# Mixer groups counted in column tiles, an input projection that begins 7 tiles wide, and the arithmetic ahead of it on VectorE alone

## The chip, the cores and the metric

One core of a Trainium2 chip runs the whole program in one launch. The metric is the device time of that launch in microseconds. Five engines work side by side, each on its own queue of instructions in a fixed order: TensorE (PE), VectorE (DVE), ScalarE (ACT), GpSimd (POOL) and SyncE (SP), which issues all of the kernel's DMAs. An instruction waits until what it reads is written and its target is free; what stands behind it on its engine waits with it.

## The reference

One layer of a decoder for 256 prompt tokens and 8 samples of one token each (264 columns), all in float32, with d_model 2048:

```python
h = h + 0.5 * rmsnorm(swiglu(rmsnorm(h, norm_ffn1_pre), ...), norm_ffn1_post)
mix, cb, xb, hs = token_mixer(rmsnorm(h, norm_mix_pre), ...)
h = h + rmsnorm(mix, norm_mix_post)
h = h + 0.5 * rmsnorm(swiglu(rmsnorm(h, norm_ffn2_pre), ...), norm_ffn2_post)
gate = jax.nn.sigmoid(rmsnorm(h, norm_ple_pre) @ w_ple_gate)
h = h + rmsnorm(gate * (p @ w_ple_proj), norm_ple_post)

def token_mixer(u, ...):
    glu_a, glu_b, z, xbc, dt_raw = split(u @ w_in)
    v = glu_a * sigmoid(glu_b)
    v, new_conv_buf = causal_dwconv(v, ...)             # 31 taps
    v = silu(layernorm(v, ...))
    xbc, new_xbc_buf = causal_dwconv(xbc, ...)          # 4 taps
    xs, bm, cm = split(silu(xbc))
    dt = softplus(dt_raw + dt_bias)
    y, h_new = ssd(xs, dt, -exp(a_log), bm, cm, d_skip, h0)   # 8 groups of 6 heads
    yg = y * silu(z)                                    # gate, RMSNorm in each group
    yg = yg * rsqrt(mean(yg * yg, per group) + EPS) * ssm_norm_g
    return concat(v, yg) @ w_out, ...
```

For the samples `ssd` is one step of the recurrence, from each sample's stored state `h0` of 48 x 64 x 128 numbers; for the prompt it runs in chunks of 128 tokens.

## The kernel before

**Matrix products.** Activations lie with features on the 128 partitions and the 264 tokens along the row, 16 tiles for d_model. Every product is made of three matmuls (`mm3`, L246): weight and activation are each split in a high half, rounded to fp32r, and the rest, and high x high, high x low and low x high are added in PSUM. The weights come as *units* in the order of `PLAN` (L71): two halves of 8 blocks of 128 x 128; each half is loaded (`wraw`), rounded on ACT (`whi`, L152) and subtracted on DVE (`wlo`, L153), at most two units ahead of use and with 4 buffers each. The activation's halves are written by `split` (L252), as tile `act`.

A *column tile* is one accumulator `acc` of 128 outputs: 16 k-tiles x 3 = 48 matmuls, one unit of weights. `gemm_one` (L346) does one; `gemm_first` (L334) starts a product four tiles wide, k by k, so that it can begin while the later activations are being made. `acc_ps` has 5 PSUM buffers, `ps` 3 for all else.

**The transition** (L487 to L523). When the first feed-forward block is done, three sums over partitions (`total`, L297) give the scale `rs`, and through `q2` the scale `r` of the mixer's input. For every k: `ys[k] * rs` (on GpSimd for the odd k above 2), addition to `H(k)` (on GpSimd but for k = 0), then the scalar form with `mix_pre` and `r`, and its split: `us`. The product with w_in follows these.

**The mixer's loop** (L810) goes over `IN_ORDER`, 81 column tiles: dt, then for each of 8 groups B, C, three x and three z, with a pair of GLU tiles in groups 1, 2, 4, 6 and the last four pairs behind the groups. `do_dt` (L552) ends in DMAs: dt and dt*a of the samples go to DRAM (`d_dt`) and come back spread over partitions (`dtp`, `eap`), and `eap` is exponentiated. `act` (L238) ties every ACT instruction that needs a function table to the one before in program order, so Silu and Exp keep the order in which they are written; a switch adds a table load (L236). `do_conv` (L610) makes B, C and x of an accumulator: three scalar forms on DVE, an addition, a Silu on ACT. `ssd` (L698) then does the group: transposes (L708), the chunked scan, and at its end the samples: the rows of B and C are transposed (L762, L763), copied (L765), stored (`d_bc`) and loaded again onto all partitions (`cbc`, L768); six pieces `h0` of the state (3 buffers) are loaded, multiplied by `cbc` on GpSimd, and reduced on DVE (L775) to `ych`. The `gate` (L790) of a group, y times Silu(z), squares added on GpSimd (`run`), their sum on PE (`total`, L300), normalisation and split, is called after the first x tile of the next group. `bg` holds the taps of the 31-tap convolution, 4 taken after each column tile.

**What sets the order.** The program is written in one sequence, and a scheduler puts each engine's instructions in a fixed order by priority (program order, unless `high_priority` moves a piece ahead) and by its own estimate of when operands are ready.

Of the kernel before, what the change touches and what calls it, by code (L numbers as in the profile page):

```python
# [19 lines left out]
P = 128  # L20
# [19 lines left out]
GLU_IN = (1, 2, 4, 6)  # L40
# [3 lines left out]
def _in_order():  # L44
# [26 lines left out]
def _plan():  # L71
# [18 lines left out]
    first = [m for _, m in IN_ORDER[:4]]  # L90
    for q in range(4):
        plan.append(("in", k16[4 * q : 4 * q + 4], first))
    for _, m in IN_ORDER[4:]:
# [32 lines left out]
class Weights:  # L126
# [9 lines left out]
    def load(self, between=()):  # L136
# [5 lines left out]
        with nullcontext() if between else tc.high_priority():  # L142
# [24 lines left out]
def kernel(ctx: ExitStack, tc: tile.TileContext, a: dict):  # L167
# [166 lines left out]
    def gemm_first(xs, kts, nunits):  # L334
        accs = [acc_tile() for _ in range(4)]
        n = 0
        total = nunits * 4
        for _ in range(nunits):
            w = ws.next()
            for kk in range(4):  # L340
                for m in range(4):
                    mm3(accs[m], w[4 * kk + m], xs[kts[n]], n == 0, n == total - 1)
                n += 1
# [12 lines left out]
    def ffn(xs, sq, done):  # L356
# [18 lines left out]
        accs = gemm_first(xs, k16, 4)  # L375
# [113 lines left out]
    rs = ffn_scale(ysq.total(), eq)  # L489

    q2 = tmp()
    tt(q2, yy.total(), rs, ALU.mult)
    stt(q2, hy.total(), 2.0, q2, ALU.mult, ALU.add)
    tt(q2, q2, rs, ALU.mult)
    stt(q2, eq, DM / EPS, q2, ALU.mult, ALU.add)
    r = rtile()
    rsqrt(r, q2, scale=1.0 / DM)
# [143 lines left out]
    def do_glu(i, pb, pa):  # L641
        if i < len(GLU_IN) + 2:
# [55 lines left out]
    def ssd(g, bf, cf, xt, ab, ea):  # L698
# [59 lines left out]
        tt(y[:, :, P:NP_], y[:, :, P:NP_], ea, ALU.add)  # L758

        js = slice(3 * g, 3 * g + 3)  # L760
# [5 lines left out]
        nc.sync.dma_start(d_bc[g].rearrange("i b n -> b i n"), rows[:NS])  # L766
        cbc = mp.tile([P, NS, P], F32, tag="cbc", bufs=1, name=nm("cbc"))
        nc.sync.dma_start(cbc, d_bc[g, 1].partition_broadcast(P))  # L768
        ych = mp.tile([P, 3, NS], F32, tag="ych", bufs=1, name=nm("ych"))
        for j in range(3):  # L770
# [368 lines left out]
```

## Time and profile before

| | |
|---|---|
| time, median of 3 runs | 2439.51 us (2439.47 to 2445.9) |
| the profiled execution | 2438.53 us, its span 2436.7 us |
| PE, DVE, ACT, POOL busy | 2370.0, 1577.0, 1181.7, 349.8 us |
| mean granted TensorE clock | 0.993 |
| DMA | 489.89 MB, 201 GB/s |

The share of the span in 40 equal slices of 61 us, in tenths; the mixer's tiles run from the thirteenth slice to the twenty-fourth:

```profile
PE   8999999999999999999999999899999999999988
DVE  6554455545557858979798975866555565565595
ACT  6444444433456465565655555544444443344464
POOL 2500000000015212121121011400000000000142
```

PE has work almost always; DVE is near its limit in some of the mixer's slices, GpSimd is mostly free, and ACT is at about half.

### The profile page before, as it was taken

Reading aid. Unit: us, or ns where it says so; the run is one execution under the profiler, and the core shown is the slowest. Engines: PE = TensorE matmul, PEld = TensorE weight load, DVE = VectorE, ACT = ScalarE, POOL = GpSimd, SP = SyncE. Lnnn points to the kernel's source line nnn. Section 1 sums busy time; section 2 is a strip of 40 time slices with the busy share of each in tenths; the row PEclk is TensorE's granted clock in tenths of the full one; section 3 lists DMA queues with packets and bytes.
Section 4 is the critical chain, followed back from the end, with each engine's and each line's share of the span. In section 5 each row is a group of like instructions: output and inputs, shape, how many; then the busy total and the mean of one; then the engine's idle time right before and its main releaser. Section 6 shows DMA issues by size and latency. Waiting matters only on the chain.

```text
span 2436.7 us, 47389 instructions
## 1 busy us (share of the span) xinstructions
PE 2370.0 (97%) x19444; PEld 2343.4 (96%) x19444; DVE 1577.0 (65%) x2273; ACT 1181.7 (48%) x1765; POOL 349.8 (14%) x351
## 2 busy tenths in 40 slices
PE   8999999999999999999999999899999999999988
PEld 8999999999999899999999999899999999999988
DVE  6554455545557858979798975866555565565595
ACT  6444444433456465565655555544444443344464
POOL 2500000000015212121121011400000000000142
PEclk9999999999999999999999999999999999999999
DMA  7656555555556666676666556477766676676653
GB/s 245 215 184 184 183 183 183 183 184 183 184 170 207 210 197 191 208 222 204 205 215 197 181 178 226 139 239 235 232 208 226 227 241 217 217 234 203 192 177 132
DMA packets 165386, 489.89 MB, mean 201 GB/s; under 512 B 25472, under 2 KB 42544, under 8 KB 165168
## 3 DMA queue, kind: packets, MB, share of 16 engines
q1 hardware_dynamic: 165168, 486.86, 62.1%
q8 instruction: 152, 2.49, 0.4%
q14 instruction: 66, 0.54, 0.1%
HBM read 465.65 MB, written 22.42 MB: 200 GB/s over the span
## 4 chain that ended last, share of the span: by engine, by line
PE 81%; DVE 7%; DMA 4%; issue 3%; ACT 2%; POOL 1%; SPq 0%; POOLq 0%; ACTq 0%; DVEq 0%
PE acc L248 26%; PE acc L249 26%; PE acc L250 26%; DVE wlo L153 3%; DVE y L217 1%; DMA d_bc<-rows 1%; DMA cbc<-d_bc 1%; POOL h L214 1%; DMA s<-in_hst 1%; DMA h<-in_hst 1%; DVE h L214 1%; DVE tmp L217 1%; ACT whi L152 1%; POOL run L214 1%; DVE act L217 1%
## 5 line engine op out<-in xcount | busy, mean ns | idle before, releaser
L250 PE MATMUL acc<-act,wlo 128*128 128x264 f32 x6320 | 1796.6, 285 | 4.4 <-DVE wlo L153 4.2
L249 PE MATMUL acc<-act,whi 128*128 128x264 f32 x6320 | 1783.7, 283 | 14.7 <-DVE act L217 7.8
L248 PE MATMUL acc<-act,whi 128*128 128x264 f32 x6320 | 1767.6, 283 | 16.6 <-ACT whi L152 8.7
L153 DVE TENSOR_TENSOR wlo<-wraw,whi 128x1024 fp32r<-128x1024 f32 (+1 forms) x806 | 994.9, 1236 | 584.9 <-ACT whi L152 580.7
L152 ACT CAST whi<-wraw 128x1024 fp32r<-128x1024 f32 (+1 forms) x806 | 829.0, 1033 | 945.2 <-PE acc L249 698.4
L248 PEld LDWEIGHTS acc<-act,whi 128*128 128x128 f32 x6320 | 1191.8, 190 | 19.9 <-ACT whi L152 8.9
L249 PEld LDWEIGHTS acc<-act,whi 128*128 128x128 f32 x6320 | 1188.6, 188 | 20.4 <-DVE act L217 10.0
L250 PEld LDWEIGHTS acc<-act,wlo 128*128 128x128 f32 x6320 | 1187.3, 188 | 8.1 <-DVE wlo L153 6.1
L214 POOL TENSOR_TENSOR run<-run,tmp 128x264 f32<-128x264 f32 x135 | 129.6, 960 | 956.0 <-ACT tmp L241 952.5
L214 POOL TENSOR_TENSOR s<-s,eap 128x1024 f32<-128x1024 f32 x24 | 46.4, 1932 | 598.8 <-DMA s<-in_hst 598.8
L217 DVE SCALAR_TENSOR_TENSOR y<-v,vec,y 128x251 f32<-128x251 f32 (+23 forms) x240 | 117.3, 512 | 1.2
L217 DVE SCALAR_TENSOR_TENSOR s<-bb,xds,s 128x128 f32<-128x128 f32 x192 | 52.6, 347 | 72.8 <-POOL s L214 72.8
L214 POOL TENSOR_TENSOR h<-h,cbc 128x512 f32<-128x512 f32 x48 | 72.2, 1524 | 167.4 <-DMA cbc<-d_bc 79.6
L256 ACT CAST act<-tmp 128x264 fp32r<-128x264 f32 x120 | 48.7, 411 | 72.8 <-DVE tmp L214 58.5
L214 DVE TENSOR_TENSOR tmp<-acc,rr 128x264 f32<-128x264 f32 x104 | 44.8, 431 | 56.8 <-PE acc L250 56.8
L214 DVE TENSOR_TENSOR tmp<-tmp,acc 128x264 f32<-128x264 f32 x88 | 37.7, 428 | 40.4 <-PE acc L250 39.4
L214 DVE TENSOR_TENSOR act<-tmp,act 128x264 fp32r<-128x264 f32 x120 | 54.3, 458 | 0.0
L241 ACT ACTIVATE tmp<-tmp 128x264 f32<-128x264 f32 x112 | 47.1, 422 | 10.2 <-DVE tmp L214 9.7
L241 ACT ACTIVATE tmp<-y 128x264 f32<-128x264 f32 x67 | 28.1, 426 | 43.6 <-DVE y L214 42.5
L214 DVE TENSOR_TENSOR y<-y,acc 128x264 f32<-128x264 f32 x80 | 34.0, 425 | 23.5 <-PE acc L250 23.5
L775 DVE TENSOR_REDUCE ych<-h 128x4 f32<-128x512 f32 x48 | 32.5, 678 | 20.0 <-POOL h L214 20.0
L217 DVE SCALAR_TENSOR_TENSOR act<-h,vec,act 128x264 fp32r<-128x264 f32 x48 | 35.2, 756 | 6.1 <-ACT act L241 6.1
(155 smaller groups left out, 787.2 us busy)
## 6 DMA issues: line engine op xcount, KB each, us to landing
wraw<-in_w SPq DMA_DIRECT2D x774, 512.0 KB, 4.7
h<-in_hst SPq DMA_DIRECT2D x48, 256.0 KB, 4.0
s<-in_hst SPq DMA_DIRECT2D x24, 512.0 KB, 6.8
out_nss<-s SPq DMA_DIRECT2D x24, 512.0 KB, 2.8
wraw<-in_w SPq DMA_DIRECT2D x32, 256.0 KB, 3.9
ab<-d_cs SPq DMA_DIRECT2D x16, 384.0 KB, 4.8
cbc<-d_bc SPq DMA_DIRECT2D x8, 512.0 KB, 4.3
bb<-d_bc SPq DMA_DIRECT2D x8, 512.0 KB, 8.3
```

What stands on the lines that cost most here:

```text
L152: nc.scalar.copy(hi, raw)
L153: nc.vector.tensor_tensor(out=lo, in0=raw, in1=hi.bitcast(F32), op=ALU.subtract)
L214: return (eng or nc.vector).tensor_tensor(out=out, in0=in0, in1=in1, op=op)
L217: return nc.vector.scalar_tensor_tensor(out=out, in0=in0, scalar=scalar, in1=in1, op0=op0, op1=op1)
L241: i = nc.scalar.activation(out=out, in_=in_, func=func, bias=bias, scale=scale)
L248: nc.tensor.matmul(acc, hi, x[:, 0, :], start=first, stop=False)
L249: nc.tensor.matmul(acc, hi, x[:, 1, :], start=False, stop=False)
L250: nc.tensor.matmul(acc, lo, x[:, 0, :], start=False, stop=last)
L256: nc.scalar.copy(t[:, 0, :], x)
L775: nc.vector.tensor_reduce(out=ych[:, j, b : b + 4], in_=h0, op=ALU.add, axis=AX.X)
```

## The change

It does five things.

1. The product with w_in begins with 7 column tiles instead of 4 (`FIRST_IN`), in 8 units of 2 k-tiles x 7 blocks. Two of the accumulators come from `ps`, five from `acc_ps`. The first seven tiles are dt, B, the three z of group 0, C and the first x: group 0's z moves ahead of its C.
2. Each group is an object `Group` whose steps are entered at column tiles counted from its C tile: the sample rows at C, `cbc` two tiles later, three thirds of the state's products (GpSimd) a tile apart from the third tile on, with the reductions of each third one step after its products; the scan a tile after the last x; the samples' result at C + 6 or two tiles after x; then the gate in two steps: the product with Silu(z) and the squares, and one tile later their sum and the rest.
3. GLU pairs stand in groups 1, 3 and 5, so that five are left behind the groups.
4. The transition's 15 additions and 7 multiplications on GpSimd go to DVE.
5. Priorities: the chain of scales after the first block has precedence, and so have the first two input tiles; the weight loads' priority is moved by a fixed offset of 1000.

```diff
@@
+FIRST_IN = 7
-GLU_IN = (1, 2, 4, 6)
+GLU_IN = (1, 3, 5)
@@ _in_order
+        z = [("z", MT_Z + 3 * g + j) for j in range(3)]
         out.append(("B", MT_BM + g))
+        if g == 0:
+            out.extend(z)
         out.append(("C", MT_CM + g))
         out.append(("x", MT_X + 3 * g))
         if g in GLU_IN:
             pair()
         out.extend(("x", MT_X + 3 * g + j) for j in (1, 2))
-        out.extend(("z", MT_Z + 3 * g + j) for j in range(3))
+        if g:
+            out.extend(z)
@@ Weights.load
-        with nullcontext() if between else tc.high_priority():
+        with nullcontext() if between else tc.high_priority(offset=1000):
@@ gemm_first
-        accs = [acc_tile() for _ in range(4)]
+        accs = [ps_tile([P, T]) if m < nm - 5 else acc_tile() for m in range(nm)]
@@ the transition
+    with tc.high_priority():
+        rs = ffn_scale(ysq.total(), eq)
...
+        rsqrt(r, q2, scale=1.0 / DM)
@@
-            tt(t, ys[k], rs, ALU.mult, nc.gpsimd if k % 2 and k > 2 else nc.vector)
-            tt(H(k), H(k), t, ALU.add, nc.gpsimd if k else nc.vector)
+            tt(t, ys[k], rs, ALU.mult)
+            tt(H(k), H(k), t, ALU.add)
         if k >= 2:
-            t = tmp()
-            stt(t, H(k - 2), V("mix_pre", k - 2), r, ALU.mult, ALU.mult)
-            us.append(split(t))
+            with tc.high_priority() if k < 4 else nullcontext():
+                t = tmp()
+                stt(t, H(k - 2), V("mix_pre", k - 2), r, ALU.mult, ALU.mult)
+                us.append(split(t))
@@ the samples, cut out of ssd
+    def sample_state(g, j, cbc, ych):
+        while products:
+            o, h0 = products.pop(0)
+            nc.vector.tensor_reduce(out=o, in_=h0, op=ALU.add, axis=AX.X)
+        if j == 3:
+            return
+        for b in range(0, NS, 4):
+            h0 = mp.tile([P, 4, P], F32, tag="h0", bufs=3, name=nm("h0"))
+            nc.sync.dma_start(h0, a["hst"][3 * g + j][:, b : b + 4, :])
+            tt(h0, h0, cbc[:, b : b + 4, :], ALU.mult, nc.gpsimd)
+            products.append((ych[:, j, b : b + 4], h0))
@@ gate, in two
+    def gate_begin(g, y, zs):
         tt(y, y, zs, ALU.mult)
         sq = SumSq(3, direct=0)
         for j in range(3):
             sq.add(y[:, j, :])
+        return sq
+
+    def gate_end(g, y, sq):
         t = tmp()
         rsqrt(t, sq.total(), eps1, 1.0 / 384)
@@ Group.__init__
+            at(place[("x", MT_X + 3 * g)], self.decays)
+            at(c, lambda: sample_rows(g, *self.pair()))
+            at(c + 2, self.sample_c)
+            for j in range(4):
+                at(c + 3 + j, lambda j=j: self.state(j))
+            at(x + 1, self.ssd)
+            out = max(c + 6, x + 2)
+            at(out, self.out)
+            begin = max(out, z) + 1
+            at(begin, self.begin)
+            at(begin + 1, self.end)
@@ the loop
-    first = gemm_first(us, k16, 4)
+    first = gemm_first(us, k16, 8, FIRST_IN)
...
+        for step in steps.pop(n, ()):
+            step()
```

Lines of the changed kernel's helpers lie 7 further down: `mm3` is L255 to L257 there, the `act` helper L248, the weight casts L159 and L160, `total` L307; the sample rows are transposed at L774 and L775 and reduced at L791.

**ACT, around the exponential of `eap`.** In these rows `eap`, `dte` and `cd` are results of `do_dt`, `bc` is B (and C) of group 0, `h` is x or z. Before:

```order
L591 COPY acs<-ps_9601 128x96
L599 COPY tmp_9613<-ps_9610 48x256
L241 ACTIVATE eap<-eap 128x192
L241 ACTIVATE dte<-dte 128x96
L241 ACTIVATE cd<-ps_9601 128x48
L236 ACT_TABLE_LOAD
L241 ACTIVATE bc_9616<-bc_9616 128x264 x2
L241 ACTIVATE h_9633<-h_9633 128x264
L236 ACT_TABLE_LOAD
```

And now:

```order
L625 COPY xo_9812<-acc_9869 128x11
L601 COPY acs<-ps_9796 128x96
L609 COPY tmp_9808<-ps_9805 48x256
L248 ACTIVATE eap<-eap 128x192
L248 ACTIVATE dte<-dte 128x96
L248 ACTIVATE cd<-ps_9796 128x48
L243 ACT_TABLE_LOAD
L248 ACTIVATE bc_9811<-bc_9811 128x264
L248 ACTIVATE h_9821<-acc_9331 128x264
L248 ACTIVATE h_9821<-acc_9332 128x264
L248 ACTIVATE h_9821<-acc_9333 128x264
```

Before, only the Silu of B and C and of the first x (`bc`, `h`) stand behind the exponential, and then a weight cast. Now the three z (read from their accumulators `acc`) stand there too.

**PE, behind the first pass.** `tm` and `tri` belong to `do_dt`. The first row below is the end of the eighth column tile (x, the second of group 0), which is the only one between the first pass and these rows. Waits are in brackets. Now:

```order
L257 MATMUL acc_9869<-act_9304,wlo_8_9668 128x264
L599 MATMUL ps_9796<-tm,tri 128x48 [waits DMAHW1_49,DMAHW7_49,Activation_49,Pool_49]
L600 MATMUL ps_9796<-tm,ones 128x48
L599 MATMUL ps_9796<-tm,tri 128x48
L600 MATMUL ps_9796<-tm,ones 128x48
L607 MATMUL ps_9805<-tri,tm 48x128 x2
L774 MATMUL ps_9832<-ident,bc_9811 8x128 [waits PE_49,Activation_49]
L255 MATMUL acc_9940<-act_9190,whi_0_9715 128x264 [waits Activation_49]
L256 MATMUL acc_9940<-act_9190,whi_0_9715 128x264
```

The transpose of B's sample rows (L774) and then the ninth column tile, whose accumulator is the first to be one that held a z, stand right behind that tile and the small matmuls of dt. Before, five column tiles and most of a sixth (B of group 1, below) stood between the first pass and L708, the transposes of x, the first that wait for such a Silu:

```order
L248 MATMUL acc_10098<-act_9262,whi_8_9982 128x264
L249 MATMUL acc_10098<-act_9262,whi_8_9982 128x264
L250 MATMUL acc_10098<-act_9262,wlo_8_9983 128x264
L708 MATMUL ps_9802<-ident,h_9633 128x128 [waits PE_49,Activation_49]
L708 MATMUL ps_9811<-ident,h_9633 128x128 [waits PE_49]
L722 MATMUL ps_9820<-bc_9616 128x128 [waits DVE_49]
```

**PE and DVE in the groups.** `run` is the sum of squares of a gate. The sum for group 1 and the sample rows of group 2 on PE, before (two places, the second 212 rows, or 4.4 tiles, later):

```order
L248 MATMUL acc_11603<-act_9278,whi_8_11356 128x264
L249 MATMUL acc_11603<-act_9278,whi_8_11356 128x264
L300 MATMUL ps_11171<-run_11162,ones 128x264 [waits Pool_49]
L708 MATMUL ps_11490<-ident,h_11153 128x128
L708 MATMUL ps_11499<-ident,h_11153 128x128 [waits PE_49]
```

```order
L248 MATMUL acc_11875<-act_9270,whi_8_11744 128x264
L762 MATMUL ps_11555<-ident,bc_11009 8x128 [waits DVE_49]
L763 MATMUL ps_11555<-ident,bc_11009 8x128
L249 MATMUL acc_11875<-act_9270,whi_8_11744 128x264
L250 MATMUL acc_11875<-act_9270,wlo_8_11745 128x264
```

and now:

```order
L255 MATMUL acc_11304<-act_9262,whi_8_11148 128x264
L307 MATMUL ps_11112<-run_11031,ones 128x264 [waits PE_49,Pool_49]
L774 MATMUL ps_11132<-ident,bc_11021 8x128 [waits PE_49]
L775 MATMUL ps_11132<-ident,bc_11021 8x128
L256 MATMUL acc_11304<-act_9262,whi_8_11148 128x264
L257 MATMUL acc_11304<-act_9262,wlo_8_11149 128x264
```

The rows come out right behind the sum. On DVE the first reductions of group 2 (`ych`) stand thus, before:

```order
L153 TENSOR_TENSOR wlo_0_11948<-wraw_0_11946,whi_0_11947 128x1024
L217 SCALAR_TENSOR_TENSOR y_11341<-v_11335,vec,y_11341 128x234
L217 SCALAR_TENSOR_TENSOR bc_11863<-acc_11875,vec,bc_11863 128x254
L775 TENSOR_REDUCE ych_11563<-h_622_11564 128x4
L217 SCALAR_TENSOR_TENSOR y_11341<-v_11335,vec,y_11341 128x233
L153 TENSOR_TENSOR wlo_8_11954<-wraw_8_11952,whi_8_11953 128x1024
L217 SCALAR_TENSOR_TENSOR bc_11863<-acc_11875,vec,bc_11863 128x253
L775 TENSOR_REDUCE ych_11563<-h_623_11568 128x4
```

and now:

```order
L224 SCALAR_TENSOR_TENSOR y_10484<-v_10478,vec,y_10484 128x228
L224 SCALAR_TENSOR_TENSOR y_10484<-v_10478,vec,y_10484 128x227
L791 TENSOR_REDUCE ych_11372<-h_598_11373 128x4
L224 SCALAR_TENSOR_TENSOR y_10484<-v_10478,vec,y_10484 128x226
L791 TENSOR_REDUCE ych_11372<-h_599_11376 128x4
L160 TENSOR_TENSOR wlo_8_11313<-wraw_8_11311,whi_8_11312 128x1024
L791 TENSOR_REDUCE ych_11372<-h_602_11444 128x4
```

Before, one reduction stood between two weight subtractions, with convolution taps around it; now two reductions stand ahead of one weight subtraction and a third behind it.

More of the change, by code (lines that the diff above doesn't have):

```diff
@@ L89, in _plan @@
         plan.append(("pp", [0, 1], list(range(8 * q, 8 * q + 8))))
[L90 to L93, printed above, removed]
+    first = [m for _, m in IN_ORDER[:FIRST_IN]]
+    for q in range(8):
+        plan.append(("in", k16[2 * q : 2 * q + 2], first))
+    for _, m in IN_ORDER[FIRST_IN:]:
         plan.append(("in", k16, [m]))
@@ L809, with at, last, group @@
+    steps = {}
+    def at(n, step):
+        steps.setdefault(n, []).append(step)
+    yctx = ctx.enter_context(ExitStack())
+    yp = None
+    def last():
+        nonlocal yp
+        mctx.close()
+        yp = yctx.enter_context(tc.tile_pool(name="yp", bufs=1))
+    first = gemm_first(us, k16, 8, FIRST_IN)
+    groups = {}
+    def group(g):
+        if g not in groups:
+            groups[g] = Group(g)
+        return groups[g]
     nglu = 0
     for n, (kind, m) in enumerate(IN_ORDER):
-        acc = first[n] if n < 4 else gemm_one(us, k16)
+        acc = first[n] if n < FIRST_IN else gemm_one(us, k16)
@@ L850 @@
                 bg.popleft()()
+    assert not steps
     for k in range(CM + 16, CM + 24):
```

110 lines of the change are left out of this document (58 added, 52 removed).

## The prediction

> **What bounds the kernel now.** I read the page first, then the windows around the one region that the diff touches, then PE's waits there.
>
> ```profile
> PE 2370.0 (97%) x19444; PEld 2343.4 (96%) x19444; DVE 1577.0 (65%) x2273; ACT 1181.7 (48%) x1765; POOL 349.8 (14%) x351
> PE 81%; DVE 7%; DMA 4%; issue 3%; ACT 2%; POOL 1%; SPq 0%; POOLq 0%; ACTq 0%; DVEq 0%
> L153 DVE TENSOR_TENSOR wlo<-wraw,whi 128x1024 fp32r<-128x1024 f32 (+1 forms) x806 | 994.9, 1236 | 584.9 <-ACT whi L152 580.7
> ```
>
> PE is busy for 2370.0 of 2436.7 us and carries 81% of the chain. The number of its matmuls does not change, so the change can only win or lose PE's stops and its half-clock stretches. The windows say where those are (columns: window; length, busy time of PE, PEld, DVE, ACT, POOL; granted clock; DMA).
>
> ```profile
> 760.00:780.00 20.00, 19.65 (x155) 18.83 (x153) 15.17 (x20) 13.76 (x25) 10.42 (x12) 1.00 0.65 205
> 780.00:800.00 20.00, 16.14 (x111) 15.31 (x110) 17.92 (x27) 13.22 (x30) 11.47 (x13) 0.91 0.87 289
> 800.00:820.00 20.00, 17.18 (x123) 16.44 (x122) 20.00 (x28) 8.34 (x15) 10.66 (x12) 0.91 0.60 209
> 820.00:840.00 20.00, 20.00 (x169) 20.00 (x168) 16.73 (x31) 11.64 (x23) 0.00 (x0) 1.00 0.61 199
> 840.00:900.00 60.00, 56.37 (x440) 53.69 (x439) 31.70 (x54) 37.52 (x74) 1.58 (x2) 0.94 0.61 178
> 900.00:1360.00 460.00, 442.85 (x3615) 428.78 (x3615) 393.66 (x678) 266.47 (x484) 96.95 (x74) 0.99 0.66 205
> ```
>
> At full speed PE starts 169 matmuls in 20 us: one each 0.118 us. I count a loss as idle time plus the clock's shortfall. **Transition** (760 to 820): 7.0 idle, and 0.09 of 40 us, is 10.6. **dt** (840 to 900): 3.6 idle and 0.06 of 60 is 7.2. **Mixer groups** (900 to 1360): 17.2 idle, and two dips of the clock, each 1.8 like that in the row of 780, make 20.8. Nothing else of PE's losses lies where the change reaches. Who PE waits for between 760 and 1360 us:
>
> ```profile
> PE ps L300 <- POOL run L214: 12.7, 9, 3.5
> PE acc L249 <- DVE act L214: 6.0, 4, 1.9
> PE ps L708 <- ACT h L241: 3.6, 2, 3.2
> PE acc L250 <- DVE wlo L153: 3.1, 4, 1.2
> ```
>
> A stop costs a little more than its row: the matmul before it drains for 0.28 us where its successor would have come at 0.118, so 0.16 each.
>
> **A. The transition: 7 column tiles wide, and GpSimd's arithmetic on DVE.** Four tiles wide, PE uses up one k-tile of the activations in 12 matmuls, 1.42 us; seven wide in 21, 2.48 us. What DVE takes for one:
>
> ```profile
> L153 DVE TENSOR_TENSOR wlo<-wraw,whi 128x1024 fp32r<-128x1024 f32 x17 | 23.7, 1393 | 3.1 <-ACT whi L152 3.1
> L217 DVE SCALAR_TENSOR_TENSOR tmp<-h,vec,rr 128x264 f32<-128x264 f32 x16 | 12.1, 761 | 0.0
> L214 DVE TENSOR_TENSOR act<-tmp,act 128x264 fp32r<-128x264 f32 x16 | 9.1, 596 | 0.0
> L214 POOL TENSOR_TENSOR h<-h,tmp 128x264 f32<-128x264 f32 x15 | 14.2, 954 | 6.1 <-DVE tmp L214 5.9
> 790.71 0.76 PE L248 MATMUL acc<-act,whi 128*128 128x264 f32 x4 [0.61 <-ACT act L256]
> 792.80 0.39 PE L249 MATMUL acc<-act,whi 128*128 128x264 f32 x1 [1.33 <-DVE act L214]
> 832.87 1.20 DVE L153 TENSOR_TENSOR wlo<-wraw,whi 128x1024 fp32r<-128x1024 f32 x1
> 834.01 0.47 DVE L217 SCALAR_TENSOR_TENSOR h<-acc,vec,h 128x255 f32<-128x255 f32 x1
> 834.40 0.14 DVE L214 TENSOR_TENSOR h<-h,shist 128x8 f32<-128x8 f32 x1
> ```
>
> These are the groups of 776 to 836 us, two rows of PE's timeline, and three of DVE's. Before: 0.76 + 0.60 + half a weight subtraction (0.70) is over 2.0 us against PE's 1.42, so PE must wait. After: 15 additions and 7 multiplications leave GpSimd, so that each k has three plain operations and one with a scalar, and 7/8 of a weight subtraction. From start to start, with GpSimd idle (820 to 840 above), DVE takes 1.14 for the subtraction and 0.39 for the scalar form (832.87, 834.01, 834.40); a plain one I take at 0.35, an estimate from these. That is 0.39 + 3 x 0.35 + 1.00 = 2.44, just under 2.48: PE is fed. The two operations that GpSimd did beside DVE are paid here, 0.70 a k, and the wider pass is what hides them; without it, 16 k-tiles would lose 16 x (1.95 - 1.42) = 8. What stays is the start. The first low half came at 792.80, after stops that sum to 1.9; now two more weight subtractions (2.3) stand ahead of it, and seven high-half matmuls in place of four cover 0.36 more: 3.9. With one half-clock window (3.4 us long, 1.7 lost) and the 0.6 of the first row that there was before, 6.2 remains of 10.6 plus 6 stops x 0.16, 11.6: **-5.4**. Bounds: -1, if DVE is a tenth slower (16 x 0.24 = 4), to -9, if the first stop stays as it was.
>
> **B. dt: a new wait.** The path of before, in the timelines of DVE, SP and ACT:
>
> ```profile
> 831.14 0.28 DVE L558 TENSOR_SCALAR h<-h 48x264 f32<-48x264 f32 x1
> 845.16 0.35 DVE L570 TENSOR_SCALAR h<-h,na 48x264 f32<-48x264 f32 x1
> 845.15 0.34 SPq L573 DMA_DIRECT2D d_dt<-h  x1
> 851.27 4.34 SPq L577 DMA_DIRECT2D eap<-d_dt  x2
> 859.99 0.36 ACT L241 ACTIVATE eap<-eap 128x192 f32<-128x192 f32 x1 [5.96 <-DMA eap<-d_dt]
> 860.63 1.28 ACT L236 ACT_TABLE_LOAD   x1
> 861.92 0.74 ACT L241 ACTIVATE bc<-bc 128x264 f32<-128x264 f32 x2
> 862.56 0.41 ACT L241 ACTIVATE h<-h 128x264 f32<-128x264 f32 x1
> ```
>
> From the store of dt to the exponential of `eap` lie 14.8 us of two DMA trips, and 2.3 more to the first Silu of B. ACT's order is fixed through that exponential: all Silu stand behind it. Before, PE had whole column tiles to run meanwhile, and stopped 3.2 us at the transposes L708. Now the three z tiles and B stand in those Silu, z holds three accumulators until then, and the transposes of the sample rows (L774) stand in PE's order right behind tile 7. So after the end E of the first pass PE has one tile only, of 48 x 0.12 = 5.8 us. E is followed by the operations of dt and the convolutions on DVE: 9 scalar forms (3.6), one weight subtraction (1.1), the reciprocal (1.7) and smaller ones, together some 7.3 us; plus 14.8 and 2.3 gives E + 24.4, and the Silu of the first z follows at once. PE has run 5.8 and 0.6 of small matmuls of it: 18 idle. Afterwards a part of the clock's next window, 2.5 lost (the 0.06 of 60 us above was 3.4 after a 3.2 us stop). 20.5 less 7.2 is **+13.3**. Bounds: +9, if the two trips take their landings alone (11 us), to +24, if dt's steps on DVE, of which the first can come at E + 3.7, spread over the 14.0 us that they took before (831.14 to 845.16).
>
> **C. The gates leave the critical path.** Eight of the nine waits of L300, 12.4 us and 8 x 0.16, belong to the sum of squares that PE reaches before GpSimd has added it. The product with z now stands one tile (5.8 us) ahead of its sum. In PE's order I count 2.1 to 2.8 tiles from the product to the sum where there were 1.5 to 1.8; the longest need before, its lead plus its stop, was 2.15. Groups 0 and 7 keep about 0.95 each: 13.7 to 1.9, **-11.8**, and the two dips of the clock that they caused, **-3.6**. Bounds: -8 (half the waits stay) to -17.
>
> **D. What is late next.** The sample rows leave PE right behind that sum, and the first reduction of the GpSimd products stands in DVE's queue a tenth of a tile after, where 0.85 tile lay between. In group 5 of before:
>
> ```profile
> 1196.95 0.27 PE L762 MATMUL ps<-ident,bc 128*8 128x128 f32 x1
> 1197.76 0.30 SPq L766 DMA_DIRECT2D d_bc<-rows x1
> 1202.64 0.34 SPq L768 DMA_DIRECT2D cbc<-d_bc x1
> 1208.17 0.69 DVE L775 TENSOR_REDUCE ych<-h 128x4 f32<-128x512 f32 x1 [0.79 <-POOL h L214]
> 1209.35 1.21 DVE L153 TENSOR_TENSOR wlo<-wraw,whi 128x1024 fp32r<-128x1024 f32 x1
> L214 POOL TENSOR_TENSOR h<-h,cbc x48: 1281/1302/2354, 899.2 to 1332.8; 128x512 f32<-128x512 f32 x48
> ```
>
> Rows to first reduction: 11.2 us, nearly all of it two DMA trips and one GpSimd product, which nothing here shortens. Behind the waiting reduction on DVE stands the weight subtraction of the next tile but one, and behind it PE. In groups 2 to 7 PE needs it 1.9 to 2.2 tiles after the rows, 11.5 to 13 us; it is done at 11.2 + 0.6 + 1.14 = 12.9, and with a second product (1.3) ahead of it at 14.2. I get 4 to 5 us in group 2 (two reductions ahead, row shown in the order above), 1.3 to 2.5 in groups 3 to 6, 2.5 in group 7, and 1 for groups 0 and 1: **+14**. The four old waits of wlo go, 3.1 + 0.6: **-3.7**. For the clock I take two windows, **+3.6**. Bounds of all this: -4 to +22.
>
> ```profile
> 1166.00:1176.00 10.00, 7.80 (x51) 7.48 (x50) 7.23 (x10) 7.07 (x12) 2.96 (x2) 0.83 0.80 252
> 980.00:990.00 10.00, 8.70 (x71) 8.37 (x70) 10.00 (x19) 6.71 (x14) 1.99 (x2) 1.00 0.69 225
> L236 ACT ACT_TABLE_LOAD  x27: 1283/1283/1283, 0.8 to 2423.2; - x27
> ```
>
> These windows say what a stop does to the clock: 2.2 us idle took it to 0.83 over the 10 us, 1.3 us idle left it at 1.00. So I expect it of the stops in groups 2 and 7 and not of the others. The Trainium skill, "TensorE: Matmul & The Clock Gate", section "Why this matters for your kernels", asks more: one idle window, about 3.4 us, before the clock halves. By that rule group 7's stop costs no clock, and the sum would be 1.8 lower; the row of 1166 to 1176 speaks against it.
>
> **Edits at nothing.** Twelve more table loads, 12 x 1.28 = 15.4 us on ACT, spread over the groups, where ACT is busy 266 of 460 us: hidden, at worst +3 where one stands ahead of a weight's cast. The scale's precedence moves a chain of some 3 us that the rows put ahead of 790.7 already: 0, at best -1. Two DMAs more on SP, and the longer priority offset of the weight loads, change the order of issues but no wait of PE that the rows show: 0. The last GLU convolutions: five pairs behind the groups in place of four, so 30 more DVE operations of 0.4 us, 12 us, later on; the sums of the layer norm still stand four units (24 us) ahead of their first use: 0.
>
> **Sum.** -5.4 + 13.3 - 11.8 - 3.6 + 14 - 3.7 + 3.6 = +6.4, on the profiled execution's 2438.5 us (span 2436.7, and 1.8 around it that stay): 2444.9. The median of 2439.5 is 1.0 above that execution, so I say **2446**.
>
> **The rivals.** (1) *The reductions never hold up PE*, since DVE has cleared its queue when they come due. For it: DVE is busy 394 of 460 us only. Against: the queue is in order, and the 11.2 us are DMA time. D falls to -3.7: 2446 - 14 - 3.6 = 2428. (2) *dt stays mixed with weight work on DVE.* In before its steps took 14.0 us on DVE, with a weight subtraction between nearly every two. For each microsecond that they end behind E + 7.3, PE idles one more, and from E + 8.1 on the result is over 0.3% slower; at E + 17.7 it is 2456. Against: the order now has one subtraction inside it, where seven stood. (3) *The gates are still waited for*, because the additions on GpSimd queue behind products of the samples, 1.3 us each and up to 2.35 while DVE works: then C gives 4 in place of 15.4, 2457. (4) *Short stops leave the clock alone*, as the cited rule has it for a stop under a window, and group 2's falls under it if its two reductions split it: no window in D, 2442.
>
> **Chances.** Forecast 0.42 (0.24 of it within 0.3%, 0.18 slower, since it lies close to that bound), rival 1 0.17 (0.14 faster), rival 2 0.18 (slower), rival 3 0.13 (0.10 slower), rival 4 0.10 (within). 0.3%, 7.3 us, is about what a measurement of this kernel can tell from no change: 2432.2 to 2446.8. Faster 0.14, same 0.40, slower 0.46. The range leaves out the lower half of rival 1 and the upper parts of 2 and 3: 2429 to 2458; that of the forecast alone is 2440 to 2452.
>
> **What would show it.** A: between 795 and the end of the first pass, near 835, PE without stops on DVE. B: one stop of 14 us or so on L774 or on the matmul behind it, ended by an ACT Silu. C: the waits of the total on GpSimd at 2 us or less. D: PE waits on wlo of 10 us or more, and reductions that wait for GpSimd right ahead of them. Wrong would be a stop in B under 8 us, or wlo waits that stay near 3.

## The result, and the profile after

The changed kernel takes 2454.61 us (median of 8 runs, 2451.8 to 2467.84) where the kernel before, on the same chip, takes 2440.84 (8 runs, 2436.42 to 2445.9): a ratio of 1.0064, 95% interval 1.0049 to 1.0079. The profiled execution is the longest of the eight, 2467.84 us with a span of 2466.1; what sets it apart comes below. From its page, and the windows that answer to those of before:

```profile
PE 2385.3 (97%) x19444; PEld 2360.7 (96%) x19444; DVE 1571.4 (64%) x2297; ACT 1197.0 (49%) x1779; POOL 327.9 (13%) x329
PE 88%; DVE 4%; ACT 3%; DMA 3%; issue 2%; POOL 1%; SPq 0%; ACTq 0%; POOLq 0%; DVEq 0%
L160 DVE TENSOR_TENSOR wlo<-wraw,whi 128x1024 fp32r<-128x1024 f32 (+1 forms) x808 | 991.3, 1228 | 611.9 <-ACT whi L159 604.8
...
780.00:800.00 20.00, 17.29 (x127) 16.08 (x125) 15.66 (x30) 15.52 (x35) 4.51 (x5) 1.00 0.84 285
800.00:820.00 20.00, 18.33 (x130) 18.33 (x131) 20.00 (x47) 8.78 (x15) 0.00 (x0) 0.83 0.69 231
840.00:860.00 20.00, 13.94 (x98) 13.07 (x96) 12.66 (x21) 7.61 (x18) 0.00 (x0) 0.91 0.46 115
860.00:880.00 20.00, 13.13 (x88) 12.86 (x89) 3.47 (x10) 15.28 (x33) 0.00 (x0) 0.74 0.51 134
900.00:1380.00 480.00, 454.00 (x3633) 439.67 (x3632) 391.94 (x675) 285.40 (x505) 86.26 (x68) 0.96 0.63 197
```

By the measure of the prediction, idle time and the clock's shortfall, the transition (780 to 820) loses 4.4 + 3.4 = 7.8 us, dt (840 to 880) 12.9 + 7.0 = 19.9, and the groups 26.0 idle and about 19 of clock (0.04 of 480, rounded). Before, the three were 10.6, 7.2 and 20.8. The three have grown by 34 us by this measure, and by 23 in the table below; in part, half clock while PE stands still is counted twice here, so the table is the better price. PE's waits between 740 and 1400 us of the changed kernel:

```profile
PE acc L257 <- DVE wlo L160: 21.5, 7, 5.3
PE ps L774 <- ACT bc L248: 8.8, 1, 8.8
PE ps L307 <- POOL run L221: 4.5, 3, 2.7
PE acc L255 <- ACT tmp L248: 4.1, 1, 4.1
```

The sum of the gates (L307) has fallen from 12.7 to 4.5; the wait for B's Silu at L774 and the one behind the first pass are new; and the waits for weight subtractions, 3.1 before, are now the largest.

To see where time goes without a window's edges, I count PE's weight matmuls from the start, 48 to a column tile, and take the time at which PE has done 132 tiles' worth (the first block), 140 (two tiles of another small product, then six tiles' worth of the product with w_in; in the changed kernel PE runs the seventh and last of the first pass behind this without a stop), 150 (dt is done) and 220 (behind all groups and five tiles further). The table gives each stretch's length less that of the kernel before, in profiled executions; GLU tiles stand in other places in the two, so each stretch is good to about 1 us. "Time" is the median of the runs, "ratio" that against the kernel before, measured beside it.

| kernel | to 132 | 132-140 first pass | 140-150 dt | 150-220 groups | rest | time | ratio (95%) |
|---|---|---|---|---|---|---|---|
| changed | +6.8 | -4.9 | +10.4 | +17.8 | -1.0 | 2454.6 | 1.0064 (1.0049-1.0079) |
| same_again | -0.5 | -4.8 | +9.7 | +8.2 | -1.3 | 2450.1 | 1.0053 (1.0036-1.0070) |
| dt_exp_later | +7.2 | -5.3 | +5.6 | +8.8 | -1.3 | 2450.9 | 1.0053 (1.0037-1.0070) |
| reduce_later | -0.2 | -4.7 | +10.1 | +1.5 | -0.8 | 2442.2 | 1.0016 (1.0003-1.0028) |
| both_later | -0.2 | -4.4 | +6.3 | -2.1 | -0.8 | 2441.7 | 1.0012 (1.0000-1.0024) |
| gate_only | +1.0 | -0.1 | +0.6 | +0.6 | -0.9 | 2438.7 | 1.0011 (0.9996-1.0026) |
| first_acc | -0.4 | -4.3 | +1.1 | +0.2 | -1.0 | 2437.1 | 1.0001 (0.9987-1.0014) |
| four_wide | -0.2 | -2.5 | +3.2 | +9.6 | +0.5 | 2449.5 | 1.0053 (1.0039-1.0068) |
| gpsimd_back | -0.5 | -4.8 | +10.1 | +8.2 | -1.2 | 2457.5 | 1.0086 (1.0055-1.0117) |
| no_trip | +8.0 | +3.7 | +11.0 | -9.1 | -2.1 | 2445.7 | 1.0032 (1.0020-1.0045) |
| early_only | -0.6 | -4.6 | -0.8 | +7.0 | -1.5 | 2439.8 | 1.0008 (0.9997-1.0019) |
| all_groups | +8.2 | -5.2 | +1.7 | +0.1 | -1.3 | 2435.0 | 0.9996 (0.9984-1.0007) |
| all_groups_exp8 | -0.2 | -5.4 | +1.2 | -0.5 | -1.3 | 2430.8 | 0.9972 (0.9961-0.9982) |

The first column is not the change's: it lies ahead of everything that was edited, and four executions have 7 to 8 us there and the others none (see the last section). So a single profile's total says less than its columns.

### The profile page after: what moved, and what is told of

Its sections match the earlier page's. It is cut to its first block, busy times and chain, and to the rows that moved or that the text cites. A ratio compares the mean times of both kernels' runs of the same rounds, so it can differ in the third digit from the quotient of the medians.

```text
span 2466.1 us, 47412 instructions
## 1 busy us (share of the span) xinstructions
PE 2385.3 (97%) x19444; PEld 2360.7 (96%) x19444; DVE 1571.4 (64%) x2297; ACT 1197.0 (49%) x1779; POOL 327.9 (13%) x329
## 4 chain that ended last, share of the span: by engine, by line
PE 88%; DVE 4%; ACT 3%; DMA 3%; issue 2%; POOL 1%; SPq 0%; ACTq 0%; POOLq 0%; DVEq 0%
PE acc L257 29%; PE acc L256 29%; PE acc L255 28%; DVE wlo L160 1%; DMA ab<-d_cs 1%; ACT ab L248 1%; ACT whi L159 1%; DMA cbc<-d_bc 1%; DVE tmp L224 1%; PE ps L759 0%; DVE act L224 0%; POOL h L221 0%; PE ps L744 0%; DMA wraw<-in_w 0%; PE ps L307 0%
## 5 line engine op out<-in xcount | busy, mean ns | idle before, releaser
L257 PE MATMUL acc<-act,wlo 128*128 128x264 f32 x6288 | 1796.7, 287 | 22.7 <-DVE wlo L160 22.6
L255 PE MATMUL acc<-act,whi 128*128 128x264 f32 x6288 | 1770.3, 284 | 18.9 <-ACT whi L159 8.5
L160 DVE TENSOR_TENSOR wlo<-wraw,whi 128x1024 fp32r<-128x1024 f32 (+1 forms) x808 | 991.3, 1228 | 611.9 <-ACT whi L159 604.8
L159 ACT CAST whi<-wraw 128x1024 fp32r<-128x1024 f32 (+1 forms) x808 | 829.1, 1030 | 994.6 <-PE acc L256 729.5
L257 PEld LDWEIGHTS acc<-act,wlo 128*128 128x128 f32 x6288 | 1187.7, 189 | 27.2 <-DVE wlo L160 25.1
L255 PEld LDWEIGHTS acc<-act,whi 128*128 128x128 f32 x6288 | 1190.9, 190 | 22.6 <-ACT whi L159 8.7
L256 PEld LDWEIGHTS acc<-act,whi 128*128 128x128 f32 x6288 | 1188.5, 189 | 11.5 <-DVE act L224 9.9
L224 DVE SCALAR_TENSOR_TENSOR y<-v,vec,y 128x243 f32<-128x243 f32 (+23 forms) x240 | 108.5, 482 | 0.6
L791 DVE TENSOR_REDUCE ych<-h 128x4 f32<-128x512 f32 x48 | 32.5, 676 | 31.0 <-POOL h L221 31.0
L248 ACT ACTIVATE tmp<-tmp 128x264 f32<-128x264 f32 x112 | 47.1, 421 | 10.2 <-DVE tmp L221 10.1
L248 ACT ACTIVATE tmp<-y 128x264 f32<-128x264 f32 x67 | 28.0, 425 | 42.9 <-DVE y L221 41.8
```

The source lines that it names most:

```text
L159: nc.scalar.copy(hi, raw)
L160: nc.vector.tensor_tensor(out=lo, in0=raw, in1=hi.bitcast(F32), op=ALU.subtract)
L224: return nc.vector.scalar_tensor_tensor(out=out, in0=in0, scalar=scalar, in1=in1, op0=op0, op1=op1)
L248: i = nc.scalar.activation(out=out, in_=in_, func=func, bias=bias, scale=scale)
L255: nc.tensor.matmul(acc, hi, x[:, 0, :], start=first, stop=False)
L256: nc.tensor.matmul(acc, hi, x[:, 1, :], start=False, stop=False)
```

## The experiments

**same_again.** The changed kernel once more, nothing edited.

> The changed kernel unaltered, for a second profile and for the spread. If the profiled execution of 2467.8 us was one with more stops than usual in the mixer groups, a second one of about 2454 shows the same stop of 14 us in the dt step (the sum of both stops 12 to 15) and fewer or shorter waits for wlo (under the 21.5 us of the first profile), or fewer dips of the clock. If the two agree within 3 us in every stretch, the spread lies elsewhere. Time 2452 to 2458.

2450.07 us. Its windows, and its waits from 740 to 1400 us:

```profile
820.00:900.00 80.00, 67.59 (x526) 65.46 (x525) 47.95 (x79) 42.03 (x81) 11.32 (x7) 0.91 0.63 187
900.00:1380.00 480.00, 456.40 (x3712) 442.97 (x3713) 401.80 (x700) 291.05 (x514) 87.89 (x68) 0.98 0.62 200
...
PE acc L257 <- DVE wlo L160: 20.5, 8, 5.3
PE ps L774 <- ACT bc L248: 8.3, 1, 8.3
PE ps L307 <- POOL run L221: 3.3, 3, 2.5
```

The waits are those of the first profile to within 1.2 us each. What the first had more is the clock's loss in the groups, 0.96 there and 0.98 here, and the 7 us ahead of the change: of what was expected, it is the fewer dips of the clock. I take this execution as the one to compare with from here on.

**dt_exp_later** writes the exponentials behind the Silu of B and z.

```diff
 def do_dt(acc):
-        act(eap, eap, AF.Exp)
...
-        act(dte, dte, AF.Exp)
-        act(cd, pc[:, 1, 1, :], AF.Exp)
+        exps.append(pc)
...
+    at(6, dt_exps)     # the three of them, ahead of group 0's decays
```

> The exponentials of eap, dte and cd are written six tiles later, at the first x of group 0, behind the Silu of B, C and the three z; nothing else changes. Theory (PE waits in the dt step because those Silu stand behind the DMA trips of eap): the wait of 8.8 us at L774 goes, PE's loss between 840 and 880 falls from 18 to 20 us to 4 to 8, and the time by 10 to 14, to 2441 to 2445. Rival (PE would wait there anyway, for the accumulators that dt and the convolutions hold): loss stays over 14, time 2451 to 2456.

2450.94 us: no gain in the time. PE's waits from 740 to 900 us, and the window beside that of same_again above:

```profile
PE acc L255 <- ACT tmp L248: 4.1, 1, 4.1
PE acc L257 <- DVE wlo L160: 3.4, 1, 3.4
PE ps L724 <- ACT h L248: 1.3, 1, 1.3
...
820.00:900.00 80.00, 71.19 (x554) 69.14 (x555) 56.06 (x91) 44.89 (x86) 10.51 (x7) 0.96 0.64 196
```

The wait at L774 is gone, as the theory has it, and the loss from 820 to 900 fell from 12.4 + 7.2 to 8.8 + 3.2 us, 7.6 less. But a wait for a weight subtraction and one for x came in its place (the dt stretch of the table is shorter by 4.1 only), and the groups keep their 8 to 9. The expected 10 to 14 was wrong. The time says no gain; in this profile 7.2 of its us lie ahead of the change, so about 4 us of gain is what the profile shows and the time cannot confirm.

**reduce_later** writes the products and reductions one tile later.

```diff
-                at(c + 3 + j, lambda j=j: self.state(j))
+                at(c + 4 + j, lambda j=j: self.state(j))
...
-            out = max(c + 6, x + 2)
+            out = max(c + 7, x + 2)
```

> The state's products and reductions are written one tile later in each group (from the fourth tile after C, not the third), and the samples' result with them. By the order the next weight subtraction behind a first reduction is then needed 2.9 to 4.2 tiles after the rows in groups 3 to 7 (2.2 to 2.4 before), and 2.2 in group 2. Theory (reductions at the head of DVE's queue hold the weight subtraction that PE needs): PE's waits for wlo fall from 21.5 us to under 6, dips of the clock with them, and the time by 12 to 22, to 2433 to 2443. Rival (the gate, which now follows a tile later, becomes the wait, or weights are late for another reason): waits for wlo under 8 but those of the sum L307 over 10, or wlo waits over 15; time 2450 to 2458.

2442.18 us, 8 below the changed kernel; the groups went from +8.2 to +1.5.

```profile
PE acc L257 <- DVE wlo L160: 10.0, 6, 6.6
PE ps L718 <- ACT h L248: 4.1, 4, 1.7
PE ps L307 <- POOL run L221: 4.1, 6, 1.2
```

The waits for wlo halved, and their longest, 6.6, is in group 2, which by the order had not moved (2.2 tiles). The gain is under the 12 to 22 expected: x (L718) waits 4.1 us that it did not before. The theory stands, its size does not.

**both_later**, the two edits together.

> Both edits at once. If the two losses are separate, as the first theories have it, the gains add: 22 to 36 less than the changed kernel, 2419 to 2432, which is faster than the kernel before by 0.4 to 0.9%. If removing one only lets the other take its place, the gain is no more than the larger of the two alone.

2441.67 us. Dt +6.3, groups -2.1: in the profile both gains are there, but the time is that of reduce_later alone. It did not reach the 2419 to 2432 expected. The 4 us that dt_exp_later wins in its stretch are at the limit of what these runs tell.

**gate_only** takes the kernel before, and puts a tile between a gate's squares and their sum.

```diff
             if j == 0:
-                finish_gate()
+                begin_gate()     # product and squares
                 ab, ea = decays(g)
+            elif j == 1:
+                finish_gate()    # sum, normalisation, split
```

> The kernel before, with one part of the change alone: a gate's product with Silu(z) and its squares stay where they were, and their sum on PE and the rest follow one column tile later. Where the sample rows and reductions stand does not change. Theory (the waits of the sum for GpSimd were worth 13.7 us and two dips of the clock, and the reductions cost the changed kernel what it won here): PE's waits at L300 between 900 and 1360 fall from 12.4 us to under 4, those for wlo stay near 3, and the time is 9 to 16 below the kernel before, 2422 to 2430. Rival (any delay of the gate brings the waits elsewhere, to x or the next wlo): gain under 4.

2438.65 us, 1.0011 of the kernel before: no change.

```profile
PE ps L300 <- POOL run L214: 8.8, 7, 2.1
PE acc L250 <- DVE wlo L153: 6.2, 7, 1.9
```

The sum's waits fell by 3.9 only, from 12.7, and those of wlo rose by 3.1. In five of the eight groups the product with Silu(z) still starts only 3.9 to 4.4 us ahead of its sum (3.6 to 5.0 in the kernel before), so there the edit did not make the distance it was written to make. It does not tell what the gates are worth alone, but it is a first case of one wait that takes the place of another.

**first_acc** is both_later with three of the first seven accumulators in the small pool.

```diff
-        accs = [ps_tile([P, T]) if m < nm - 5 else acc_tile() ...
+        accs = [ps_tile([P, T]) if m < nm - (4 if nm > 4 else 5) else acc_tile() ...
```

> Both later edits, and three of the first seven accumulators come from the small PSUM pool in place of two, so that one of the five large buffers is free when the first pass ends. Theory (the stop of 4.1 us behind the first pass is for an accumulator): that stop goes, and the time is 3 to 5 below both_later, 2436 to 2439. Rival (the dt step is bound by its own chain, or the small pool holds up dt's transposes): another stop of 3 us or more takes its place, time within 2 of both_later.

2437.11 us, 4.6 below both_later (2.7 by the two ratios, which were measured on their own sets of runs and whose intervals overlap). The profile is clearer: the stop of 4.1 us behind the first pass is gone, and dt fell from +6.3 to +1.1. That stop was for an accumulator, and cost what it showed and a little clock.

**four_wide** is the changed kernel with `FIRST_IN = 4` in four units.

> The changed kernel with the first pass four tiles wide (dt, B and two z) in four units, the rest of its order unaltered, GpSimd's arithmetic still on DVE. Theory (the width hides the arithmetic moved to DVE, and the held accumulators make the stop behind the pass): the first pass is bound by DVE and loses 6 to 10 more than with seven tiles, while the step of dt loses 5 to 10 less, since more tiles lie between; time within 4 of the changed kernel's 2450. Rival (the width costs nothing and hides nothing): the loss in the first pass is equal within 2.

2449.5 us. The first pass gains 2.5 in place of 4.8, dt loses 3.2 in place of 9.7. Narrower costs 2.3 in the pass, not the 6 to 10 of the working; dt came out as expected.

**gpsimd_back** puts the 15 additions and 7 multiplications back on GpSimd.

> The changed kernel with the 15 additions and 7 multiplications ahead of the input projection on GpSimd again. Theory (seven tiles wide PE needs 2.48 us a k-tile, and DVE keeps up either way; GpSimd at work makes DVE's operations longer): the first pass ends within 2 us of the changed kernel's, time 2448 to 2454. Rival (moving them off GpSimd is what won the 5 us): the first pass ends 3 or more later.

2457.5 us, above the 2448 to 2454 expected: the median of four runs, from 2450.1 to 2459.0. In the profile every stretch is that of same_again, the first pass too (-4.8 both). So by the profile the move off GpSimd is worth nothing, and the 7 us in the median are not located; the interval of the ratio, 1.0055 to 1.0117, overlaps that of same_again, and since profiles differ by 7 us ahead of the change, they stay open.

**no_trip** loads the operand of the products from elsewhere, so that it need not go through DRAM; the samples' y is left out by that.

```diff
-        nc.sync.dma_start(cbc, d_bc[g, 1].partition_broadcast(P))
+        nc.sync.dma_start(cbc, a["hst"][3 * g])
```

> The changed kernel, with the operand of the samples' products loaded from the stored state instead of from the rows of C that were just written to DRAM: the same bytes, no trip through DRAM ahead of them. The samples' y is left out by this (it is computed with other numbers). Theory (reductions wait 11 us for that trip at the head of DVE's queue): PE's waits for wlo fall from 20.5 us to under 6, the reductions' idle time ahead of them from 31.0 to under 10, and the time from 2450 to 2432 to 2440. Rival (DVE has too much to do in these stretches, and the weight subtraction would be late in any order): wlo waits stay over 12, time over 2445.

2445.66 us, above what was expected, but the columns tell why. In the groups it is 17.3 us faster than same_again (-9.1 against +8.2). Between 740 and 1400 us:

```profile
PE acc L257 <- DVE wlo L160: 4.6, 5, 1.6
PE ps L307 <- POOL run L221: 7.0, 5, 2.1
PE ps L257 <- DVE wlo L160: 3.4, 1, 3.4
```

The wlo waits behind the first pass are 4.6 in place of 20.5 (the 3.4 us are in the pass, two of whose accumulators are called `ps`). What the reductions wait for GpSimd fell to 10.8 us, a little over the 10 expected, from 31.0 in the first profile. Group 0's products, freed of their wait, were scheduled into the first pass, and made it 8.5 us longer, with GpSimd at work beside DVE. So the trip through DRAM ahead of the reductions is what the groups lose to: shown.

**early_only** is the kernel before with its groups as they were and the change's early part, with the two mends (accumulators, exponentials).

> The kernel before, mixer groups as they were, with the change's early part only: seven tiles wide, group 0's z first, no GpSimd, precedence for the scale and the first inputs, the weight loads' offset; and with the two mends found here (three accumulators from the small pool, the exponentials of dt at the first x). Theory (the first pass wins 5 us, the mends keep the step of dt from losing them, and what the changed kernel loses lies in its groups): 4 to 7 below the kernel before, 2429 to 2433, with PE's waits at L300 still 11 to 14. Rival (the step of dt takes back what the first pass wins, whatever the groups do): within 2 of the kernel before.

2439.79 us, 1.0008 (0.9997 to 1.0019). First pass -4.6, dt -0.8, as expected; but the groups lost 7.0.

```profile
PE ps L307 <- POOL run L221: 17.4, 9, 6.2
PE acc L257 <- DVE wlo L160: 1.9, 4, 0.8
```

The longest wait, 6.2, is that of group 0's gate, which waited 3.5 in the kernel before. By the order, its z tiles come early and no longer stand between the scan and the sum, so PE reaches the sum before GpSimd has added it. The rival is nearer: what the pass won was taken back, mostly around group 0's gate and not in the step of dt. The early part alone wins nothing without gates that are later.

**all_groups** is first_acc with delays of 2, 3, 3, 1, 1, 1, 1 and 1 tiles in place of 1 for all; **all_groups_exp8** moves the exponentials to the third x as well (`at(8, dt_exps)`).

> first_acc, with the delay of the samples' products chosen for each group (2, 3, 3, 1, 1, 1, 1, 1 tiles) so that by the order the weight subtraction behind a first reduction is needed at least 2.9 tiles after the rows in groups 2 to 7; group 1 stays at 2.25. Theory (the remaining wlo waits of first_acc, 11.5 us, are the reductions of groups 1 to 3): wlo waits fall to 4 to 7, the time 3 to 7 below first_acc, 2430 to 2434, which is 0.1 to 0.4% below the kernel before. Rival (another engine's queue takes the place of each wait that is removed): wlo falls, but x, gate or cast waits grow by as much, time within 2 of the kernel before.

> The same, with the exponentials of dt written two tiles later still (at the third x), so that no weight cast stands behind the DMA trip of eap; it adds a table load. Theory (the 2.1 us stop near 875 is a cast behind that exponential): that stop goes, 1 to 3 below all_groups. Rival: the transposes of x, which follow, wait instead; time within 1.

2434.96 and 2430.83 us. The second, at 0.9972 (0.9961 to 0.9982) of the kernel before, beats both kernels: by 5.2 us the one, by some 20 the changed one. Its longest waits on weights and x:

```profile
PE acc L257 <- DVE wlo L160: 8.0, 9, 3.6
PE ps L724 <- ACT h L248: 5.2, 6, 1.4
PE acc L255 <- ACT whi L159: 3.1, 2, 2.1
```

The waits for wlo are 12.6 us in all_groups, no less than in first_acc (11.5), and 8.0 here, while x and casts wait 8.3 together. The 2.1 us stop near 875 was to go and is still there, at 2.1. So neither expectation's mechanism is confirmed, and what separates the two times (4 us, where all_groups' profile again has 8 us ahead of the change) stays open; the gain on the kernel before is measured. By its columns it comes from the first pass, -5.4, and not from the groups, -0.5.

## Why the prediction was right, and where not

The forecast was 2446 (2429 to 2458), leaning to slower; 2454.6 and 2450.1 lie inside, on that side. The profile of same_again is 11.4 us over that of before (2449.94 against 2438.53), where the sum said +6.4. By the table that closeness is in part luck: dt came out 3.6 below its forecast and the groups 9.7 above theirs.

**A, the transition**, was right in size: -5.4 forecast, -4.8 and -4.9 found. The working behind it was not. The arithmetic moved to DVE was to cost 8 us if the pass were narrow (by its own terms 9: 0.39 + 3 x 0.35 + half of 1.14 is 2.01 us a k, not 1.95), and the width to hide it: four_wide lost 2.3, and gpsimd_back gained and lost nothing. Why DVE keeps up so much better than its summed durations say was not settled. What brings the remaining 2.5 us, the precedences or the order of the first inputs, was not tried alone.

**B, dt**, was right in kind and too large: the stretch costs 9.7 to 10.4 us more than before, where 13.3 were forecast. Counted as loss it is 19.6 to 19.9 of 20.5, but from idle time of 12.4 to 12.9 rather than 18, and clock of 7 rather than 2.5, of which PE stood still for part. The one stop of 14 us that was to show it came as two, 4.1 and 8.3. In same_again the path from dt to the Silu is as it was read from before, in DVE's, SP's, PE's and ACT's timelines:

```profile
836.52 0.29 PE L257 MATMUL acc<-act,wlo 128*128 128x264 f32 x1
840.89 0.56 PE L255 MATMUL acc<-act,whi 128*128 128x264 f32 x1 [4.09 <-ACT tmp L248]
841.25 0.42 PE L256 MATMUL acc<-act,whi 128*128 128x264 f32 x1
841.47 0.42 PE L257 MATMUL acc<-act,wlo 128*128 128x264 f32 x1
844.45 0.35 DVE L580 TENSOR_SCALAR h<-h,na 48x264 f32<-48x264 f32 x1
844.37 0.34 SPq L583 DMA_DIRECT2D d_dt<-h  x1
856.52 0.36 ACT L248 ACTIVATE eap<-eap 128x192 f32<-128x192 f32 x1 [5.51 <-DMA eap<-d_dt]
858.45 0.42 ACT L248 ACTIVATE bc<-bc 128x264 f32<-128x264 f32 x1
```

The first pass ends at 836.8. DVE ends dt 8.0 us later, where 7.3 were forecast; the two trips take 12.2, not 14.8; B's Silu follows at E + 21.7. The one tile in between starts 4.1 us late, a stop that the forecast did not have, and its first matmuls run at half clock, 0.22 us each (841.25, 841.47): that fills time that I had counted as idle. Rival 2 (dt mixed with weight work) fell, though dt's end lies just short of the E + 8.1 that it named. As shown by first_acc, the 4.1 us are the accumulators'; the wait at L774 is the Silu behind `eap`, since it went when these were moved, though other waits then took half of what it had cost.

**C, the gates**: right in kind, a little large. L307 waits for 3.3 to 4.5 us, not 1.9, so 8 to 9 us of wait went, not 11.8. What is left is mostly group 1's sum (2.5 us in same_again), not groups 0 and 7, which were to keep 0.95 each. Rival 3 fell.

**D, what is late next**, is the step that was mis-sized, and with it the groups: forecast about -1.5 us net, found +8.2 and +17.8. The mechanism is the one told: no_trip shows it, and reduce_later agrees. It was taken at 14 us and two windows of the clock; it is 20.5 to 21.5 us of waits, and the clock lost about 9.6 (0.02 of 480) to 19 us. Group by group, the starts of PE's matmuls in same_again give 4.9 us in group 2 (forecast 4 to 5), but 5.5 and 5.0 in groups 3 and 5, where 1.3 to 2.5 were forecast. Group 3 in the timelines of GpSimd and DVE:

```profile
1036.27 3.95 POOL L221 TENSOR_TENSOR h<-h,cbc 128x512 f32<-128x512 f32 x3 [12.30 <-DMA cbc<-d_bc]
1037.60 0.69 DVE L791 TENSOR_REDUCE ych<-h 128x4 f32<-128x512 f32 x1 [6.67 <-POOL h L221]
1038.20 2.31 DVE L221 TENSOR_TENSOR act<-tmp,act 128x264 fp32r<-128x264 f32 x2
1040.43 0.67 DVE L791 TENSOR_REDUCE ych<-h 128x4 f32<-128x512 f32 x1
1041.01 1.56 POOL L221 TENSOR_TENSOR h<-h,cbc 128x512 f32<-128x512 f32 x1 [0.79 <-DMA h<-in_hst]
1041.03 0.42 DVE L221 TENSOR_TENSOR act<-tmp,act 128x264 fp32r<-128x264 f32 x1
1041.37 2.28 DVE L160 TENSOR_TENSOR wlo<-wraw,whi 128x1024 fp32r<-128x1024 f32 x1
```

The first reduction waits 6.67 us; then come two splits that take 2.31 us together, where the third (1041.03, as GpSimd begins its next) takes 0.42, a second reduction, and the weight subtraction at 2.28 in place of the 1.23 of the page's mean. GpSimd's products run from 1036.27 to 1040.22 and from 1041.01 to 1042.57, just then. I had priced what stands behind a late reduction at DVE's speed alone, and had counted two reductions but not the splits between. The price with GpSimd at work was in the rows that I quoted (1.39 as a mean for the subtraction, 0.60 for the split's half, in the transition), and its neighbours are worse. Over the whole of same_again, no weight subtraction took over 1.23 us while GpSimd was idle; beside it some took up to 2.31, and others still 1.21. So GpSimd at work goes with the long ones, but no run varied that alone.

**Rival 1**, that the reductions never hold up PE, fell with no_trip. The reductions of the kernel before waited too, but oftener and for less; between 900 and 1380 us, before and in same_again:

```profile
DVE ych L775 <- POOL h L214: 20.0, 19, 2.9
DVE ych L791 <- POOL h L221: 25.9, 8, 6.7
```

Rival 4 holds that short stops leave the clock alone. The Trainium skill has it so in "TensorE: Matmul & The Clock Gate" ("Why this matters for your kernels"): one idle window halves the clock, which "Part 1" of that page puts at about 3.4 us. The rival fell in the first profile. Two of its windows, and one of same_again:

```profile
980.00:1000.00 20.00, 16.07 (x113) 15.65 (x113) 16.67 (x28) 10.76 (x16) 8.00 (x6) 0.88 0.44 153
1120.00:1140.00 20.00, 19.58 (x150) 19.58 (x151) 18.74 (x27) 7.94 (x13) 6.27 (x4) 0.91 0.84 262
...
980.00:1000.00 20.00, 15.45 (x126) 15.03 (x125) 19.86 (x29) 7.05 (x11) 4.68 (x4) 1.00 0.71 240
```

The starts of PE's matmuls have two stops of 2.2 and 2.1 us in the first of these windows, and one of 2.0 just ahead of the second; each time the clock fell. So 2 us can be enough. They need not be: in the third, same_again's group 2, stops of 1.1 and 3.4 us left the clock at 1.00. What decides it is open, and so is how often it falls, which is where the two profiles of one kernel differ in the groups. The clock's loss there is larger than I took it because I expected it of two stops alone.

**Edits at nothing**: the last column is -1.0 to -1.3, and same_again has no wait of PE between 1300 and 1400 us, where the five pairs stand, so the tail costs nothing, as said. What the twelve table loads cost was not measured alone.

## What to carry to other kernels

Where one engine's queue is in order, look behind each instruction that waits for a DMA trip, and price what stands there at the speed it has while the producer is at work: here some of it took twice as long. An edit that takes a wait off the critical path (the gates, 12.7 to 4.5 us) is worth that only if the steps that it pulls forward do not now arrive ahead of their own data; the same groups lost it with their reductions, and got 6.7 us back when these were written later. And a wide first pass should leave one accumulator free for the tile behind it: here the stop for one, 4.1 us, took back most of the 4.8 that the pass had won.

## What the runs showed that was not expected

The 600 us from 100 to 700 hold the same instructions in all these kernels, without idle time and at full granted clock. Here are the first profile of the changed kernel and that of same_again:

```profile
100.00:700.00 600.00, 600.00 (x4957) 600.00 (x4956) 302.68 (x329) 243.11 (x294) 13.31 (x26) 1.00 0.57 181
100.00:700.00 600.00, 600.00 (x5002) 600.00 (x5001) 305.90 (x334) 246.51 (x298) 12.27 (x25) 1.00 0.56 182
```

In the first, PE gets through 45 matmuls fewer of 5000, 0.9%, at the same clock and with no stop that the profile shows: they start 121.1 ns apart on the mean, and 120.0 in same_again. dt_exp_later, all_groups and no_trip have 4956 or 4957 too, all the others 5002 or 5003, nothing between. From 820 us on the difference is gone in three of the four; in no_trip it lasts to 900 at least, which makes its columns of the first pass and of dt about 0.5 us each too large. Runs of every kernel but reduce_later, the one before included, lie 7 us or more apart (2432.64 to 2446.99 in one set of 24); this is likely one part of it, though only profiled executions show where it lies. No cause was found.
